# Attention outputs divided head by head, the first convolution tap on ScalarE, and four buffers for the backward states' loads

## The chip, the cores and the metric

The kernel runs on one core of a Trainium2 chip. The metric is the device time of one execution in microseconds, and of several executions the median. Everything is float32 in DRAM; matmul operands are split into a high and a low part (hi and lo), and three matmuls (hi hi, hi lo, lo hi) stand for one product of float32.

## The reference

One layer of a hybrid encoder block over 1024 tokens of width 1024. What matters here, cut down:

```
q, k, v, xBC, z, dt_raw, gates = split(h @ w_in)
# branch A, 16 heads of 64, 4 key heads
sc = einsum("bqgrd,bkgd->bgrqk", q, k) * scale
p = softmax(sc, axis=-1)
attn = einsum("bgrqk,bkgd->bqgrd", p, v)
# branch B
xBC = silu(depthwise_conv_centred(xBC, conv_w, conv_b))   # 5 taps, 3072 channels
ssd = ssd_mixer(...)                                       # chunked scan, forward and backward
merged = sigmoid(g_A) * (attn @ w_attn_out) + sigmoid(g_B) * (ssd @ w_ssd_out)
x = x + gate1 * (merged @ w_o)
...                                                        # then an MLP with squared relu
```

The softmax's division by the row sum is done on the output: the kernel forms exp(score - max) and its row sums, multiplies the unnormalised weights with v, and multiplies each output by the reciprocal of its row sum later.

## The kernel before, in words

The work runs through stages one after another, all in one program: modulation, the projections of q, k, v and z, then the three stages that the change touches, then the merge, w_o and the MLP. TensorE has most of the work. A scheduler puts the instructions of each engine in order when the program is built, from the order of the code and a timeline of its own; in attention and in the scan stage the order on TensorE alone is that of the code (manual_schedule), where weave mixes two streams by their costs. Each engine and each DMA queue works strictly in its order.

*Convolution stage (about 425 to 735 us).* 12 pairs of channel blocks of xBC, and one pair of gate blocks. A pair is one Strassen-Winograd step of the projection: its weights come in two loads, r0 (two buffers) and r1 (one buffer, so the next pair's load waits until the last reader of this one is through); GpSimd forms four sums of weight blocks (ws); each of seven operands is split into hi (ScalarE) and lo (VectorE for the plain blocks, GpSimd for the sums), both under the name wop, in four buffers; seven products of 12 matmuls follow (psc). VectorE and GpSimd add these into two rows pa and pb (both called pad, 1024 tokens and two zeros at either end). Then conv runs for pb and for pa: five taps. The first is L712 (pad times weight plus bias) and the other four are L715 (accumulator cacc plus shifted pad times weight), all five on VectorE; ScalarE applies SiLU in place, and a pair later TensorE turns the result to token order, eight transpositions that ScalarE copies out and stores to DRAM.

*Attention (about 735 to 1240 us).* 16 heads of 8 units of 128 queries. scores(u): four matmuls to pss, VectorE's negated row maximum (nm, L893), ScalarE's exponential (pf, L895) which also leaves the row sums in column u of zall. turn(u, hf): four transpositions (L906) to pst (two buffers), split into ph on ScalarE and pl on VectorE. values(b, hf), for blocks of four units: matmuls into pv (one buffer), whose two halves ScalarE (ax, L930) and VectorE (av) add up; av goes unnormalised to DRAM (av_d). Gate products (psg) are woven between. After the last unit, zall is turned at once, its reciprocals are formed, and stored to rz_d.

*Scan stage (from about 1240 us).* TensorE's order has the remaining gate products, the backward states of group 0 (bwd_stream: load xbb, two buffers, GpSimd's product xdb, one matmul, VectorE's update prevb, store pb), the scan of the chunks, and the product of attention's output with w_attn_out. load_a brings that output: for 16 tiles a load of av_d (araw, three buffers), two loads of rz_d that repeat a head's reciprocals over 64 partitions (rz, two buffers), VectorE's product, and the split into ah and al. All these loads stand in SP's one queue, which waits at an instruction whose buffer isn't free.

Of the kernel before, what the change touches and what calls it, by code (L numbers as in the profile page):

```python
# [18 lines left out]
P = 128  # L19
S = 1024  # L20
# [71 lines left out]
def block(ctx: ExitStack, tc: tile.TileContext, ia, out, upto=99, dbg=None):  # L92
# [611 lines left out]
    with tc.tile_pool(name="p2", bufs=1, reuse_waits="tile") as p2, \  # L704
# [4 lines left out]

        def conv(i, pad):  # L710
            acc = accs.pop() if accs else acc_tile()
            V.tensor_scalar(out=acc, in0=pad[:, 0:S], scalar1=cwT[:, i:i + 1], scalar2=vecT[:, CB0 + i:CB0 + i + 1],  # L712
                            op0=ALU.mult, op1=ALU.add)
            for k in range(1, 5):
                V.scalar_tensor_tensor(out=acc, in0=pad[:, k:k + S], scalar=cwT[:, 24 * k + i:24 * k + i + 1],  # L715
                                       in1=acc, op0=ALU.mult, op1=ALU.add)
            A.activation(acc, acc, AF.Silu)
# [130 lines left out]
    with tc.tile_pool(name="p3k", bufs=1, reuse_waits="tile") as p3k, \  # L848
# [11 lines left out]
        def attn_stream():  # L860
# [49 lines left out]
            pvs = {}  # L910

            def values(b, hf):

# [14 lines left out]
                if hf == 1:  # L928
                    ax = p3.tile([HD, 512], F32, name="ax", tag="ax", bufs=1)
                    A.copy(ax, pv[HD:])  # L930
                    av = p3.tile([HD, 512], F32, name="av", tag="av", bufs=2)
                    tt(V, av, ax, pv[:HD], ALU.add)
                    dma(av_d[h // 2][(h % 2) * HD:(h % 2 + 1) * HD, (b % 2) * 512:(b % 2 + 1) * 512], av)
                yield 0.92

            def all_values(b):
# [12 lines left out]
            for u in range(NU + 4):  # L949
                if u % NT == 4 and 1 < u // NT + 1 < NH:  # L950
                    load_head(u // NT + 1)
                if u + 2 < NU:
                    scores(u + 2)
                    yield 0.92
                for hf in range(2):
                    if u < NU:
                        turn(u, hf)
                        yield 0.44
                    if hf == 0:
                        c = next(pvq, None)  # L960
                        if c:
                            yield c
                if u % 4 == 3 and u < NU:
                    pvq = all_values(u // 4)
            ps = ps3.tile([P, 4, P], F32, name="pst", tag="pst", bufs=2)
            T.transpose(ps[:, 0], zall, ident)
            zt = p3.tile([P, P], F32, name="zt", tag="pf", bufs=2)
            V.reciprocal(zt, ps[:, 0])
            dma(rz_d.rearrange("h (a b) -> (h a) b", b=P), zt)

        with tc.manual_schedule(engines=M2):
            weave(tc, (attn_stream(), 128 * 2.72 + L0), (gates_stream(p3, ps3, 0, GATES_EARLY, 1, G), GATES_EARLY * 10.4), lead=LEAD2)
# [22 lines left out]
    with tc.tile_pool(name="p4", bufs=1, reuse_waits="tile") as p4, \  # L995
# [26 lines left out]
        def bwd_stream(g):  # L1022
            hs = slice(8 * g, 8 * g + 8)
            prev = None
            for c in range(7, 0, -1):
                xb = p4.tile([P, 640], F32, name="xbb", tag="xbb", bufs=2)
                dma(xb, xb_d[g][:, c])
                xt, bt = xb[:, 0:512].rearrange("p (h d) -> p h d", h=8), xb[:, 512:640]
                xd = p4.tile([P, 8, HD], F32, name="xdb", tag="xd", bufs=3)
# [113 lines left out]
        def load_a():  # L1143
            for half in range(2):
                ns = slice(half * 512, (half + 1) * 512)
                for k in range(KT):
                    raw = p4.tile([P, 512], F32, name="araw", tag="araw", bufs=3)
                    dma(raw, av_d[k][:, ns])
                    rz = p4.tile([P, 512], F32, name="rz", tag="rz", bufs=2)
                    for j in range(2):  # L1150
                        dma(rz[j * HD:(j + 1) * HD, :], rz_d[2 * k + j, ns].partition_broadcast(HD))
                    tt(V, raw, raw, rz, ALU.mult)
                    split(ahi[k][half], alo[k][half], raw)

        ghi, glo = act_tiles("g", KT)
# [552 lines left out]
```

## Time and profile before

| what | value |
|---|---|
| median of 3 runs | 2610.28 us (2604.86 to 2614.72) |
| the profiled execution | 2610.79 us, span 2608.8 us |
| mean granted TensorE clock | 0.975 |
| convolution, 456 to 717 us: TensorE, VectorE, GpSimd busy | 234.3, 219.2, 186.4 us |
| attention, 735 to 1240 us: TensorE, VectorE, ScalarE busy | 492.8, 335.8, 329.6 us |
| start of the scan, 1240 to 1330 us: TensorE busy, share of the DMA engines | 69.9 us, 0.82 |

PE is TensorE, DVE is VectorE, ACT is ScalarE, POOL is GpSimd; SPq and ACTq are the engines' DMA queues. A busy time says how long an engine had an instruction in hand, which for VectorE and GpSimd includes time in which the one holds the other up. A row of a group has line, engine, operation, out<-in by name, shapes and count, then busy time and the mean of one in nanoseconds, then idle time of that engine just before and what ended it. A row of the timeline has its start in us from the span's start, then its length. The chain of waits is followed back from the last instruction: each piece is what the next one waited for.

### The profile page before, as it was taken

The numbers are of one execution on the slowest core, as the hardware profiler recorded it, in microseconds if no ns is written. First come the engines' busy times: TensorE is split into PE (matmuls) and PEld (weight loads), VectorE is DVE, ScalarE is ACT, GpSimd is POOL, SyncE is SP. The second block draws the span as 40 slices with busy tenths as digits, with TensorE's granted clock in tenths as the row PEclk, the third lists the DMA queues.
The fourth block names the chain that finished last, engine by engine and source line by source line (L and its number), as shares of the span: only waits on it lengthen the run. The fifth ranks groups of instructions, "written<-read, shape, count | busy, mean of one in ns | idle before, by whom it ended". The sixth has DMA issues, their size and how long they took to land.

```text
span 2608.8 us, 32331 instructions
## 1 busy us (share of the span) xinstructions
PE 2435.3 (93%) x11340; PEld 1940.2 (74%) x11340; DVE 1844.4 (71%) x2200; ACT 1105.0 (42%) x1928; POOL 1016.0 (39%) x728
## 2 busy tenths in 40 slices
PE   5999999998989999999799999998989999899995
PEld 5998777776767777777567767776777888688884
DVE  5756347888856666666487787546569888768889
ACT  5455422333346666666233444343332222364441
POOL 2310117766710000000155666424018866633356
PEclk9999999999999999999899999999999999899998
DMA  7653741323441212111866675466315544754432
GB/s 258 184 157 124 253 152 61 89 85 93 145 140 45 77 45 79 47 52 29 239 216 196 194 223 169 125 221 207 133 49 178 189 144 144 265 179 149 142 93 97
DMA packets 286788, 369.69 MB, mean 142 GB/s; under 512 B 34201, under 2 KB 167041, under 8 KB 286625
## 3 DMA queue, kind: packets, MB, share of 16 engines
q1 hardware_dynamic: 215297, 292.62, 36.3%
q10 hardware_dynamic: 71328, 74.99, 8.7%
q8 instruction: 90, 1.47, 0.2%
q14 instruction: 73, 0.60, 0.1%
HBM read 251.33 MB, written 116.20 MB: 141 GB/s over the span
## 4 chain that ended last, share of the span: by engine, by line
PE 67%; DVE 11%; DMA 8%; issue 6%; POOL 5%; ACT 2%; SPq 1%; DVEq 0%; ACTq 0%; POOLq 0%
PE pst L906 5%; PE pp L1313 4%; PE pp L1315 4%; PE pp L1314 4%; PE psq L381 4%; PE psq L382 4%; PE psq L380 4%; PE psg L207 3%; PE psg L208 3%; PE psg L209 3%; PE p L1655 3%; PE p L1656 3%; PE p L1654 3%; PE pss L889 2%; PE pss L891 2%
## 5 line engine op out<-in xcount | busy, mean ns | idle before, releaser
L893 DVE TENSOR_REDUCE nm<-pss 128x1 f32<-128x1024 f32 x128 | 156.6, 1224 | 140.1 <-PE pss L891 139.6
L381 PE MATMUL psq<-twl,hh 128*128 128x400 f32 (+1 forms) x512 | 192.9, 378 | 5.9 <-DVE twl L155 4.1
L1655 PE MATMUL p<-o,o 128*128 128x512 f32 x448 | 179.8, 401 | 19.1 <-DVE o L155 19.1
L380 PE MATMUL psq<-twh,hh 128*128 128x400 f32 (+1 forms) x512 | 192.2, 381 | 3.7 <-ACT qkvr L513 1.2
L382 PE MATMUL psq<-twh,hl 128*128 128x400 f32 (+1 forms) x512 | 191.8, 377 | 0.0
L155 DVE TENSOR_TENSOR pl<-pst,ph 128x512 fp32r<-128x512 f32 x256 | 168.4, 684 | 27.5 <-ACT ph L169 27.5
L1654 PE MATMUL p<-o,o 128*128 128x512 f32 x448 | 177.3, 399 | 9.6 <-ACT o L169 7.7
L895 ACT ACTIVATE pf<-pss,nm 128x1024 f32<-128x1024 f32 x128 | 142.8, 1115 | 101.6 <-PE pst L906 98.0
L155 POOL TENSOR_TENSOR wlo<-wraw,whi 128x1024 fp32r<-128x1024 f32 x12 | 28.7, 2390 | 399.0 <-ACT whi L169 358.3
L1656 PE MATMUL p<-o,o 128*128 128x512 f32 x448 | 177.0, 397 | 0.0
L169 ACT CAST ph<-pst 128x512 fp32r<-128x512 f32 x256 | 146.3, 585 | 51.7 <-PE pst L906 37.5
L906 PEld LDWEIGHTS pst<-masks,pf 128*128 128x128 f32 x1024 | 118.8, 140 | 66.2 <-issue 28.8
L906 PE MATMUL pst<-masks,pf 128*128 128x128 f32 x1024 | 157.0, 276 | 9.7 <-DVE pl L155 9.6
L155 POOL TENSOR_TENSOR sl<-sl 128x512 f32<-128x512 f32 x64 | 95.0, 1492 | 175.5 <-DVE o L155 83.2
L715 DVE SCALAR_TENSOR_TENSOR cacc<-pad,cwT,cacc 128x1024 f32<-128x1024 f32 x96 | 149.7, 1570 | 0.4
L169 ACT CAST o<-ar 128x512 fp32r<-128x512 f32 x112 | 69.8, 623 | 175.8 <-PE p L1656 155.2
L155 DVE TENSOR_TENSOR o<-ar,o 128x512 fp32r<-128x512 f32 x112 | 107.2, 957 | 48.1 <-ACT o L169 48.1
L169 ACT CAST wop<-ws 128x512 fp32r<-128x512 f32 x116 | 70.6, 620 | 122.7 <-PE pp L1315 69.2
L1655 PEld LDWEIGHTS p<-o,o 128*128 128x128 f32 x448 | 86.5, 193 | 41.6 <-DVE o L155 23.7
L381 PEld LDWEIGHTS psq<-twl,hh 128*128 128x128 f32 x512 | 98.5, 192 | 17.9 <-DVE twl L155 5.2
L155 DVE TENSOR_TENSOR o<-sl,o 128x512 fp32r<-128x512 f32 x112 | 111.3, 994 | 0.1
L380 PEld LDWEIGHTS psq<-twh,hh 128*128 128x128 f32 x512 | 98.0, 192 | 16.0 <-ACT qkvr L513 1.7
(416 smaller groups left out, 7166.0 us busy)
## 6 DMA issues: line engine op xcount, KB each, us to landing
ar<-r SPq DMA_DIRECT2D x112, 256.0 KB
wada<-in_w_ada_dram SPq DMA_DIRECT2D x48, 512.0 KB
r<-in_w_mlp_dram SPq DMA_DIRECT2D x32, 512.0 KB
r<-as SPq DMA_DIRECT2D x64, 256.0 KB
sl<-in_w_mlp_dram SPq DMA_DIRECT2D x64, 256.0 KB
r<-in_w_in_dram SPq DMA_DIRECT2D x26, 512.0 KB
r<-ro ACTq DMA_DIRECT2D x48, 256.0 KB
xb<-cst ACTq DMA_DIRECT2D x20, 512.0 KB
```

The lines of the kernel that those rows point to most:

```text
L155: e.tensor_tensor(out=o, in0=a, in1=b, op=op)
L169: (e_hi or A.copy)(hi, src)
L380: T.matmul(o, hhi[k][half][:, sl], hi[:, k % 2, :n], start=k == 0, stop=False)
L381: T.matmul(o, hhi[k][half][:, sl], lo[:, k % 2, :n], start=False, stop=False)
L382: T.matmul(o, hlo[k][half][:, sl], hi[:, k % 2, :n], start=False, stop=k == KT - 1)
L715: V.scalar_tensor_tensor(out=acc, in0=pad[:, k:k + S], scalar=cwT[:, 24 * k + i:24 * k + i + 1], in1=acc, op0=ALU.mult, op1=ALU.add)
L893: V.tensor_reduce(out=nm, in_=ps, axis=AX.X, op=ALU.max, negate=True)
L895: A.activation(pfs[u], ps, AF.Exp, bias=nm, accum_out=zall[:, u:u + 1])
L906: T.transpose(pt[:, k], pf[:, (hf * 4 + k) * P:(hf * 4 + k + 1) * P], ident)
L1654: T.matmul(pss[t], a[:, 0, sl], b[:, 0], start=k == 0, stop=False)
L1655: T.matmul(pss[t], a[:, 0, sl], b[:, 1], start=False, stop=False)
L1656: T.matmul(pss[t], a[:, 1, sl], b[:, 0], start=False, stop=k == KR - 1)
```

## The change

Three parts. In the convolution the first tap goes from VectorE to ScalarE (Identity with scale and bias). In attention a head's reciprocals are formed as soon as its row sums stand: a reciprocal on VectorE over eight columns, a transposition of these to 8 x 128 on TensorE in a buffer of pst, a copy and a store on ScalarE's queue, one unit later a load over 64 partitions (rz, one buffer), and in the two units after that GpSimd multiplies the two halves of the head's output, which are then stored. load_a loads finished values and only splits them; the transposition of zall at the end goes. The backward states' load xbb gets four buffers instead of two.

```
-            V.tensor_scalar(out=acc, in0=pad[:, 0:S], scalar1=cwT[:, i:i + 1], scalar2=vecT[:, CB0 + i:CB0 + i + 1],
-                            op0=ALU.mult, op1=ALU.add)
+            A.activation(acc, pad[:, 0:S], AF.Identity, scale=cwT[:, i:i + 1], bias=vecT[:, CB0 + i:CB0 + i + 1])
...
+            def sums(h):
+                zi = p3.tile([P, NT], F32, name="zi", tag="zi", bufs=1)
+                V.reciprocal(zi, zall[:, NT * h:NT * h + NT])
+                pz = ps3.tile([P, 4, P], F32, name="pst", tag="pst", bufs=2)
+                T.transpose(pz[0:NT, 0], zi, ident)
+                zr = p3.tile([NT, P], F32, name="zr", tag="zr", bufs=1)
+                A.copy(zr, pz[0:NT, 0])
+                adma(rz_d[h].rearrange("(t p) -> t p", p=P), zr)
+            def sums_back(h):
+                rzs[h] = p3.tile([HD, S], F32, name="rz", tag="rz", bufs=1)
+                dma(rzs[h], rz_d[h].partition_broadcast(HD))
+            def divide(b):
+                h, av, hs = b // 2, avs.pop(b), slice((b % 2) * 512, (b % 2 + 1) * 512)
+                tt(G, av, av, rzs[h][:, hs], ALU.mult)
+                dma(av_d[h // 2][(h % 2) * HD:(h % 2 + 1) * HD, hs], av)
...
-                    dma(av_d[h // 2][(h % 2) * HD:(h % 2 + 1) * HD, (b % 2) * 512:(b % 2 + 1) * 512], av)
+                    avs[b] = av
...
+                h = u // NT - 1
+                if h >= 0:
+                    if u % NT == 0:
+                        sums(h)
+                    elif u % NT == 1:
+                        sums_back(h)
+                    elif u % NT in (2, 3):
+                        divide(2 * h + u % NT - 2)
...
-            ps = ps3.tile([P, 4, P], F32, name="pst", tag="pst", bufs=2)
-            T.transpose(ps[:, 0], zall, ident)
-            zt = p3.tile([P, P], F32, name="zt", tag="pf", bufs=2)
-            V.reciprocal(zt, ps[:, 0])
-            dma(rz_d.rearrange("h (a b) -> (h a) b", b=P), zt)
...
-                xb = p4.tile([P, 640], F32, name="xbb", tag="xbb", bufs=2)
+                xb = p4.tile([P, 640], F32, name="xbb", tag="xbb", bufs=4)
...
-                    rz = p4.tile([P, 512], F32, name="rz", tag="rz", bufs=2)
-                    for j in range(2):
-                        dma(rz[j * HD:(j + 1) * HD, :], rz_d[2 * k + j, ns].partition_broadcast(HD))
-                    tt(V, raw, raw, rz, ALU.mult)
```

The scheduler moves more than the lines that changed. VectorE in one round of the convolution, before, from the split of the next pair's second block to the split of its last (wop from r1): cacc_4406 belongs to pb (pad_4257), cacc_4430 to pa (pad_4254).

```order
L155 TENSOR_TENSOR wop_4465<-r1_4368,wop_4465 128x512
L712 TENSOR_SCALAR cacc_4406<-pad_4257,cwT_311,vecT_312 128x1024
L715 SCALAR_TENSOR_TENSOR cacc_4406<-pad_4257,cwT_311,cacc_4406 128x1024
L155 TENSOR_TENSOR pad_4254<-pad_4254,psc_4416 128x512
L715 SCALAR_TENSOR_TENSOR cacc_4406<-pad_4257,cwT_311,cacc_4406 128x1024
L712 TENSOR_SCALAR cacc_4430<-pad_4254,cwT_311,vecT_312 128x1024
L715 SCALAR_TENSOR_TENSOR cacc_4406<-pad_4257,cwT_311,cacc_4406 128x1024
L715 SCALAR_TENSOR_TENSOR cacc_4430<-pad_4254,cwT_311,cacc_4430 128x1024
L155 TENSOR_TENSOR wop_4532<-r1_4368,wop_4532 128x512
```

The same stretch now (a pair later; cacc_4589 belongs to pb, cacc_4613 to pa):

```order
L155 TENSOR_TENSOR wop_4648<-r1_4551,wop_4648 128x512
L155 TENSOR_TENSOR pad_4437<-pad_4437,psc_4599 128x512
L714 SCALAR_TENSOR_TENSOR cacc_4589<-pad_4440,cwT_311,cacc_4589 128x1024 x2
L714 SCALAR_TENSOR_TENSOR cacc_4613<-pad_4437,cwT_311,cacc_4613 128x1024
L714 SCALAR_TENSOR_TENSOR cacc_4589<-pad_4440,cwT_311,cacc_4589 128x1024
L155 TENSOR_TENSOR wop_4715<-r1_4551,wop_4715 128x512
```

The add of the last product to pa has moved ahead of all taps, and four taps instead of five and two first taps stand between it and the split. GpSimd in the same round, before: wop_4371 and wop_4413 are the lo parts of the pair's last two sums, ws_4443 is the next pair's first sum, which waits for the load of r1.

```order
L155 TENSOR_TENSOR wop_4371<-ws_4260,wop_4371 128x512
L775 MEMSET pad_4437 128x2
L776 MEMSET pad_4437 128x2
L155 TENSOR_TENSOR ws_4443<-r0_4366,r1_4368 128x512
L155 TENSOR_TENSOR wop_4413<-ws_4404,wop_4413 128x512
L155 TENSOR_TENSOR ws_4463<-ws_4443,r0_4366 128x512
```

And now:

```order
L155 TENSOR_TENSOR wop_4371<-ws_4260,wop_4371 128x512
L155 TENSOR_TENSOR wop_4413<-ws_4404,wop_4413 128x512
L155 TENSOR_TENSOR ws_4443<-r0_4366,r1_4368 128x512
L774 MEMSET pad_4437 128x2
L775 MEMSET pad_4437 128x2
L155 TENSOR_TENSOR ws_4463<-ws_4443,r0_4366 128x512
```

The lo part wop_4413 has moved from behind the sum that waits for r1 to ahead of it. ScalarE in attention, at the first unit of the second head, before (pst are turned blocks, pf exponentials):

```order
L169 CAST ph_6659<-pst_6661 128x4x128
L895 ACTIVATE pf_6657,zall_6042<-pss_6650,nm_6655 128x1024
L169 CAST ph_6659<-pst_6707 128x4x128
L169 CAST ph_6686<-pst_6688 128x4x128
L895 ACTIVATE pf_6702,zall_6042<-pss_6695,nm_6700 128x1024
```

And now, with the transposed reciprocals in pst_6707:

```order
L169 CAST ph_6669<-pst_6671 128x4x128
L894 ACTIVATE pf_6667,zall_6042<-pss_6660,nm_6665 128x1024
L918 COPY zr_6709<-pst_6707 8x128
L919 DMA rz_93<-zr_6709 8x128
L169 CAST ph_6669<-pst_6724 128x4x128
L169 CAST ph_6696<-pst_6698 128x4x128
L894 ACTIVATE pf_6719,zall_6042<-pss_6712,nm_6717 128x1024
```

The copy and the DMA issue stand behind the exponential and ahead of the two splits of turned blocks.

More of the change, by code (lines that the diff above doesn't have):

```diff
@@ L908, in turn @@
                 split(phs[b, hf][:, :, js], pls[b, hf][:, :, js], pt)
-            pvs = {}
+            pvs, rzs, avs = {}, {}, {}
+            def sums(h):
[13 more added lines that the diff above has]
+                dma(av_d[h // 2][(h % 2) * HD:(h % 2 + 1) * HD, hs], av)
             def values(b, hf):
```

## Prediction

> **What bounds the kernel now.** I read the busy shares first, then the chain that ended last.
>
> ```profile
> PE 2435.3 (93%) x11340; PEld 1940.2 (74%) x11340; DVE 1844.4 (71%) x2200; ACT 1105.0 (42%) x1928; POOL 1016.0 (39%) x728
> PE 67%; DVE 11%; DMA 8%; issue 6%; POOL 5%; ACT 2%; SPq 1%; DVEq 0%; ACTq 0%; POOLq 0%
> ```
>
> TensorE is busy for 93% of the span, yet only 67% of the chain is its own. So there are stretches that something else ends, and only there can this change gain. The busy times by stretch show which of its stages those are: the convolution (456 to 717 us), attention (735 to 1240) and the start of the scan (1240 to 1330).
>
> ```profile
> core 0: us, PE busy (x) PEld busy (x) DVE busy (x) ACT busy (x) POOL busy (x), PEclk, DMA share, GB/s
> 456.00:717.00 261.00, 234.30 (x1054) 188.34 (x1053) 219.16 (x188) 95.23 (x159) 186.36 (x153) 0.97 0.35 103
> 735.00:1240.00 505.00, 492.82 (x2595) 377.38 (x2594) 335.84 (x415) 329.62 (x578) 29.09 (x19) 1.00 0.20 59
> 1240.00:1330.00 90.00, 69.89 (x254) 48.31 (x252) 52.39 (x75) 24.07 (x43) 20.50 (x17) 0.89 0.82 243
> 1330.00:1690.00 360.00, 353.04 (x1694) 265.00 (x1695) 263.13 (x321) 143.40 (x293) 217.17 (x160) 1.00 0.61 185
> ```
>
> The convolution leaves TensorE 26.7 us idle, attention 12.2, the start of the scan 20.1. The waits of TensorE in the convolution, then one round of the chain there:
>
> ```profile
> PE psc L770 <- DVE wop L155: 20.3, 10, 2.3
> PE psc L770 <- POOL wop L155: 6.4, 6, 2.4
> ```
>
> ```profile
> 547.20 0.61 DVE wop L155
> ...
> 547.86 1.40 DMA r<-in_w_in_dram
> ...
> 551.75 1.98 POOL ws L155
> 553.73 1.70 POOL wop L155
> ...
> 560.71 1.06 POOL pad L155
> ...
> 561.79 1.57 DVE cacc L712
> ...
> 565.51 0.67 DVE pad L155
> ...
> 567.83 1.71 DVE cacc L712
> ...
> 571.92 0.61 DVE wop L155
> ```
>
> Read it as a ring. VectorE splits the last block of a pair (wop, ending at 547.81); only then is the single buffer r1 free and loaded; GpSimd can form the sums at 551.75 (3.94 us later); it ends the first pad at 561.77 (10.02); VectorE goes through two L712, five of the other operations and the next wop, ending at 572.53 (10.76). One round is 24.7 us, and in each TensorE waits about 2 us for that wop.
>
> **The convolution.** The change takes L712 out of the third leg. These rows give the prices: first two single taps, then groups of the stage.
>
> ```profile
> 538.67 2.19 DVE L715 SCALAR_TENSOR_TENSOR cacc<-pad,cwT,cacc 128x1024 f32<-128x1024 f32 x1
> 549.52 1.27 DVE L715 SCALAR_TENSOR_TENSOR cacc<-pad,cwT,cacc 128x1024 f32<-128x1024 f32 x1
> ```
>
> ```profile
> L155 POOL TENSOR_TENSOR wop<-ws,wop 128x512 fp32r<-128x512 f32 x44 | 87.9, 2017 | 0.0
> L155 POOL TENSOR_TENSOR pad<-pad,p 128x512 f32<-128x512 f32 x22 | 23.5, 1091 | 0.0
> L717 ACT ACTIVATE cacc<-cacc 128x1024 f32<-128x1024 f32 x21 | 22.3, 1061 | 128.6 <-DVE cacc L715 128.6
> ```
>
> A tap takes 1.27 us while GpSimd idles and 2.19 beside its work; a GpSimd operation of one shape takes 1.09 or 2.02. The two engines hold each other up, so what leaves VectorE's queue isn't simply saved. New round, leg by leg. Load: 3.94 unchanged. GpSimd: 10.02, less the wop of 1.70, which the new order puts ahead of the load's wait; but VectorE's add to the second pad now stands ahead of the first tap, so the second pad (1.09) and that add (0.67) come in: 10.08. ScalarE's tap has no row; its nearest is the SiLU over the same shape, 1.06 us, and it runs beside these 1.76 us, since it needs the first pad only. VectorE: four L715 and the wop (0.61), between 4 x 1.27 and 4 x 2.19, so 5.7 to 9.4; GpSimd now has four wop in a row there, so I take three taps at 2.19 and one at 1.27: 8.45. The round is 22.5 us (19.7 to 23.4).
>
> The second bound is TensorE: its 234.3 us over 10.6 rounds are 22.2 a round. So the gain a round is at most 2.5 us, at least 1.3, and I take 2.2. Of 12 pairs, the first and last lie outside the ring: 10 x 2.2 = 22 us gained. If the ring stays (below) it is 0; if all idle time and the lost clock (3% of 261 us) go, about 34.
>
> The tap's wait for the pad is new on ScalarE. Behind it stand the cast for the next product, the second tap and the copy of c1. ScalarE is busy for 95 of 261 us, and TensorE has a product of 12 matmuls in hand by then, so I cost that wait at nothing; were the cover gone, each round would give back up to the 1.06 us.
>
> The Trainium skill (SBUF — State Buffer, Who interferes with whom) says that VectorE with two SBUF inputs, or in a two-port mode as a scalar operation can be, and GpSimd hold one port pair in turn, for a whole instruction, and that ScalarE has ports of its own. By that rule eight taps, three wop and ten GpSimd operations lie end to end: about 22.9 us a round, an estimate with the alone prices above; the gain would be 18 us instead of 22.
>
> **Attention.** Per head the change adds a reciprocal, a small TensorE transposition, a copy and a DMA issue on ScalarE, a load on SP's queue, and two products on GpSimd.
>
> ```profile
> PE pst L906 <- DVE pl L155: 9.6, 17, 1.6
> L906 PE MATMUL pst<-masks,pf 128*128 128x128 f32 x980 | 150.2, 276 | 6.0 <-DVE pl L155 5.8
> L895 ACT ACTIVATE pf<-pss,nm 128x1024 f32<-128x1024 f32 x122 | 136.1, 1115 | 94.6 <-PE pst L906 93.2 <-DVE pl L155 0.9
> L895 ACT ACTIVATION_READ_ACCUMULATOR pf<-pss,nm 128x1 f32 x122 | 23.4, 192 | 0.0
> L930 ACT COPY ax<-pv 64x512 f32<-64x512 f32 x30 | 17.5, 583 | 12.3 <-PE pv L925 12.0
> 981.80 0.36 ACTq L856 DMA_DIRECT2D gt<-ost  x1
> ```
>
> TensorE is full here, so everything on it counts. A transposition of one block is 0.28 us at most, 16 of them 0 to 4.4 us; I take 2. It also takes one of two pst buffers, free again only after ScalarE's copy (0.19 to 0.58 us), which stands behind an exponential (1.12). The next turn needs that buffer after four score matmuls, about 0.9 us. So the wait lies between nothing and 1.12 + 0.58 + 0.36 - 0.9 = 1.2 us a head, 0 to 19 us. The exponential's scores were issued a whole unit earlier, so most of its time is past: I take 0.25 us a head, 4 us. The reciprocal stands ahead of two splits in VectorE's order, four units after its data; I cost it and the GpSimd products (32 x 1.09 us at most, in 505 us with 29 busy) at nothing. The loads move 16 x 256 KB into a stage whose DMA share is 0.20; SP holds q1 loads and stores behind each, needed units later. Sum: 6 us lost (2 to 23).
>
> **The start of the scan.** TensorE's waits there, what the DMAs moved, and the queue:
>
> ```profile
> PE psg L207 <- ACT ah L169: 8.4, 3, 4.3
> PE pst L1032 <- POOL xdb L155: 5.5, 1, 5.5
> PE psd L1082 <- ACT e L1085: 3.9, 1, 3.9
> PE psg L208 <- DVE al L155: 2.6, 2, 2.1
> ...
> ```
>
> ```profile
> DMA packets 16355, 22.38 MB, mean 231 GB/s; under 512 B 1814, under 2 KB 7390, under 8 KB 16350
> ...
> rz<-rz SPq DMA_DIRECT2D x32, 128.0 KB
> ...
> 1248.33 0.45 SPq L933 DMA_DIRECT2D av<-av  x1
> 1248.87 1.03 SPq L1027 DMA_DIRECT2D xbb<-xb  x2
> ...
> ```
>
> The 32 broadcast loads are 4.2 of 22.4 MB, 18 us at 231 GB/s, and 32 of the queue's issues; they leave, as do 16 VectorE products. The waits for ah and al (11.0 us) are waits for them, and the 5.5 us for xdb are a load of xbb that stood behind rz loads in SP's queue; with four buffers the first four are issued together. That is 16.5 us. The 3.9 us for e I leave. The clock is 0.89 over 90 us, about 10 us lost to half rate after these stalls; I take 4 back. Against it, SP now waits for the last head's division before the first xbb: transposition, store, load and product in a row, 2.5 us. Sum: 18 us gained; 6 if only waits for al and half of those for ah go, 28 if stalls and clock go whole.
>
> The later xbb loads of the backward states meet a stage in which TensorE is busy 353 of 360 us: nothing.
>
> **Sum.** 22 - 6 + 18 = 34 us gained. The profiled execution took 2610.8 us (span 2608.8), the median of before is 2610.3, so the forecast needs no shift: 2577 us.
>
> **Rivals.** *The ring stays.* GpSimd's fourth wop and the taps block each other for what was freed, and the convolution gives 0: 2610.8 + 6 - 18 = 2599. For it: the 2.02 against 1.09 us; against: the leg loses two operations of 1.6 us outright. 0.10.
>
> *The start stays DMA-bound.* The loads left are 18 MB, and states wait on each other through DRAM; only 3 us come back there: 2592. 0.08.
>
> *Slower.* The new slot wait in attention. If the copy stands behind its exponential and a reduction each time and the splits behind it come late as well, TensorE loses 3.5 us a head, 56 in all, against 40 gained: 2627. It decides from 2.5 us a head. Against it: TensorE's longest wait on pst is 1.6 us now, and 9.6 us over the whole stage. 0.07.
>
> *Everything clears.* Convolution 30, start 29 with its whole clock, attention 2 lost: 2554. 0.10. Whether the clock follows is open, as a gap of one round of the convolution shows:
>
> ```profile
> 547.85 0.50 PE L770 MATMUL psc<-u4h,wop 128*128 128x512 f32 x1 [2.26 <-DVE wop L155]
> ...
> 549.07 0.63 PE L768 MATMUL psc<-u4h,wop 128*128 128x512 f32 x1
> 549.50 0.63 PE L769 MATMUL psc<-u4l,wop 128*128 128x512 f32 x1
> ```
>
> After a gap of 2.26 us the matmuls start 0.43 us apart; the stage's mean is 234.3 / 1054 = 0.22 us. The Trainium skill (TensorE: Matmul & The Clock Gate, What's actually happening) halves the clock after an idle window of about 3.4 us. By that rule gaps of 2 us would cost no clock; the trace has half rate after one, so the measurement decides.
>
> That the change doesn't do what it says is no case: each moved instruction stands in the order.
>
> **Numbers.** The forecast has 0.65. Its own range: at best all three sums at their good ends, 25 + 28 - 2, gives 2560; their bad ends together would be 38 us worse, and I let one of them, or a bit under half of each, come true: 2594. Before's fastest run lies 5 us below its median, so 3 us more go below. With the two milder rivals (2592, 2599) the range 2557 to 2600 holds 0.83; left out are 2554 and 2627. A measurement of this kernel can tell about 0.5% (13 us) from no change: 2597 to 2623 is "same". Faster: forecast, start, clearing, less tails, 0.81; same 0.13 (the ring and tails); slower 0.06.
>
> **What would show it.** Right: TensorE's wait for wop in the convolution falls from 20 us to under 8 and the taps' rounds come every 22 to 23 us; waits on ah and al vanish; attention gets 2 to 10 us longer. Wrong: the round stays at 24, or pst waits pass 40 us in attention.

## The result, and the profile after

The changed kernel takes 2582.4 us (median of 4 runs, 2578.2 to 2585.6) where the kernel before took 2609.1 beside it. The ratio is 0.9895, with an interval of 0.9869 to 0.9922. Its profiled execution has a span of 2583.3 us, before 2608.8: 25.5 us less. The forecast was 34 us less, 2577, and a range of 2557 to 2600.

To see where the 25.5 us come from, I take five marks from TensorE's timeline, the same instructions in each kernel: the first psc matmul (convolution), the first pss (attention), the last pv (end of attention), the first psy (scan under way), the first psr (merge). The stretches between the marks, in us:

| stretch | before | after | difference | forecast |
|---|---|---|---|---|
| up to the first psc | 413.9 | 415.6 | +1.7 | 0 |
| convolution, first psc to first pss | 327.4 | 308.4 | -19.0 | -22 |
| attention, first pss to last pv | 504.0 | 509.2 | +5.2 | +6 |
| start of the scan, last pv to first psy | 75.9 | 65.8 | -10.1 | -18 |
| scan, first psy to first psr | 400.8 | 399.4 | -1.4 | 0 |
| the rest | 886.8 | 884.9 | -1.9 | 0 |

The first and the last row run over the same work in every kernel of this study. They came out between 411.0 and 416.0 us and between 882.6 and 889.9 us in them, so these two rows tell nothing. The page of the changed kernel:

```profile
PE 2435.1 (94%) x11355; PEld 1942.7 (75%) x11355; DVE 1835.2 (71%) x2175; ACT 1135.0 (44%) x1968; POOL 1047.2 (41%) x760
PE 69%; DVE 11%; DMA 8%; issue 5%; POOL 3%; ACT 3%; SPq 1%; ACTq 0%; DVEq 0%; POOLq 0%
```

Over the whole execution TensorE is as busy as before (2435 us); its idle time has become less. The busy times of the stretches between the marks, of before and then of the changed kernel (stretch, its length, then busy time and count for TensorE, its weight loads, VectorE, ScalarE and GpSimd, the granted clock, the DMA engines' share and GB/s):

```profile
413.90:741.30 327.40, 292.63 (x1284) 233.84 (x1283) 269.67 (x234) 114.97 (x188) 223.39 (x180) 0.96 0.36 110
741.30:1245.30 504.00, 492.24 (x2597) 376.55 (x2596) 337.95 (x417) 329.86 (x579) 28.59 (x18) 1.00 0.19 54
1245.30:1321.20 75.90, 57.49 (x198) 39.78 (x197) 43.32 (x64) 19.52 (x34) 15.52 (x14) 0.87 0.89 263
```

```profile
415.60:724.00 308.40, 285.19 (x1284) 231.29 (x1283) 260.58 (x210) 141.52 (x212) 214.14 (x180) 0.97 0.37 114
724.00:1233.20 509.20, 495.52 (x2612) 377.15 (x2611) 340.04 (x433) 332.24 (x595) 62.27 (x40) 1.00 0.21 63
1233.20:1299.00 65.80, 56.25 (x198) 39.12 (x197) 40.12 (x51) 19.84 (x35) 26.54 (x24) 0.90 0.81 262
```

Read the third line of each: the start of the scan moves data at 263 GB/s before and at 262 after. And read the first: 1284 matmuls, the same ones, keep TensorE busy for 292.6 us before and 285.2 after. So of the 19.0 us of the convolution 7.4 are busy time, and 11.6 are idle time (34.8 before, 23.2 after). Both will matter.

**The ring of the convolution.** One of its rounds in the changed kernel, from the chain that ended last:

```profile
543.58 0.61 DVE wop L155
...
544.24 3.72 DMA r<-in_w_in_dram
...
548.03 1.47 POOL ws L155
...
549.59 4.15 POOL ws L155 x3
...
554.77 2.49 POOL pad L155 x2
...
557.28 0.69 DVE pad L155
557.97 1.62 DVE cacc L714
...
559.62 2.27 DVE cacc L714 x2
...
563.98 2.31 DVE cacc L714
566.29 0.61 DVE wop L155
```

The legs are the forecast ones, in their new order: load 544.19 to 548.03 (3.84 us; forecast 3.94), GpSimd with VectorE's add 548.03 to 557.97 (9.94; 10.08), four taps and the split 557.97 to 566.90 (8.93; 8.45). The round is 22.7 us; 22.5 was forecast. ScalarE's first taps (1.25 us each, beside the second pad and the add) are not in the chain. But not every round is like that: from one matmul after this wait to the same one ten rounds later it is 708.26 - 474.89 us, 23.3 a round. The first nine take 23.0 on the mean (from 474.89 to 682.25 us) and the last 26.0. TensorE still waits for that split in nearly each:

```profile
PE psc L769 <- DVE wop L155: 16.9, 10, 2.6
PE psc L767 <- ACT hh L169: 2.9, 1, 2.9
PE psc L769 <- POOL wop L155: 1.6, 1, 1.6
```

**Attention.** The wait for the pst buffer that holds the turned reciprocals is there and small:

```profile
PE pst L905 <- DVE pl L155: 9.6, 17, 1.6
PE pst L905 <- ACT zr L918: 1.8, 4, 0.4
```

```profile
L916 PE MATMUL pst<-masks,zi x16: 272/273/276, 761.4 to 1229.5; 128*8 128x128 f32 x16
```

1.8 us in four waits for zr (forecast 4 us), and 3.3 us more of TensorE's busy time for the sixteen transpositions (forecast 2), together the 5.2 us.

**The start of the scan.** The wait for xdb (5.5 us) is gone, those for ah and al are not:

```profile
PE psg L207 <- ACT ah L169: 4.6, 3, 2.2
PE psd L1104 <- ACT e L1107: 3.2, 1, 3.2
PE psg L208 <- DVE al L155: 1.6, 3, 1.2
```

SP's queue shows why (start, length, then the instruction):

```profile
1236.29 1.90 SPq L929 DMA_DIRECT2D av<-av  x2
1238.28 1.98 SPq L1049 DMA_DIRECT2D xbb<-xb  x4
...
1251.31 1.33 SPq L1170 DMA_DIRECT2D araw<-av  x3
```

The first load of attention's output (araw) goes out 18.1 us after the last pv matmul (1233.2). The queue first waits for the last head's division, then come the four xbb loads and the loads of the scan. TensorE waits for ah because of araw now, where before it waited because of rz.

### The profile page after: what moved, and what is told of

Same layout as the page of the kernel before. It is cut to its first block, busy times and chain, and to the rows that moved or that the text cites. A ratio compares the mean times of both kernels' runs of the same rounds, so it can differ in the third digit from the quotient of the medians.

```text
span 2583.3 us, 32423 instructions
## 1 busy us (share of the span) xinstructions
PE 2435.1 (94%) x11355; PEld 1942.7 (75%) x11355; DVE 1835.2 (71%) x2175; ACT 1135.0 (44%) x1968; POOL 1047.2 (41%) x760
## 4 chain that ended last, share of the span: by engine, by line
PE 69%; DVE 11%; DMA 8%; issue 5%; POOL 3%; ACT 3%; SPq 1%; ACTq 0%; DVEq 0%; POOLq 0%
PE pst L905 5%; PE pp L1331 4%; PE pp L1333 4%; PE pp L1332 4%; PE psg L207 4%; PE psg L208 4%; PE psg L209 3%; PE psq L381 3%; PE psq L382 3%; PE psq L380 3%; PE p L1673 3%; PE p L1674 3%; PE p L1672 3%; DVE cacc L714 3%; PE pss L888 2%
## 5 line engine op out<-in xcount | busy, mean ns | idle before, releaser
L155 POOL TENSOR_TENSOR av<-av,rz 64x512 f32<-64x512 f32 x32 | 41.2, 1288 | 326.7 <-DMA rz<-rz 167.6
L714 DVE SCALAR_TENSOR_TENSOR cacc<-pad,cwT,cacc 128x1024 f32<-128x1024 f32 x96 | 162.9, 1727 | 0.4
L1673 PEld LDWEIGHTS p<-o,o 128*128 128x128 f32 x448 | 86.4, 193 | 42.0 <-DVE o L155 24.5
```

The source lines that it names most:

```text
L155: e.tensor_tensor(out=o, in0=a, in1=b, op=op)
L1673: T.matmul(pss[t], a[:, 0, sl], b[:, 1], start=False, stop=False)
```

## The experiments

The changed kernel and each experiment had the kernel before timed beside them; ratios are to that. Stretches are those of the table above, each from one profiled execution.

**The three parts one by one.** The first tap alone, in the kernel before:

```
-            V.tensor_scalar(out=acc, in0=pad[:, 0:S], scalar1=cwT[:, i:i + 1], ...)
+            A.activation(acc, pad[:, 0:S], AF.Identity, scale=cwT[:, i:i + 1], bias=...)
```

> The kernel before with only the first tap on ScalarE. My theory: the convolution's gain is this edit's alone, and nothing else in the program moves. From the first psc matmul to the first pss matmul the changed kernel needed 308.4 us where before needed 327.4; this kernel should need 307 to 311, and its time should be 15 to 21 us under before (ratio 0.992 to 0.994). Rival: part of those 19 us comes from the other edits, through the weights and gates loaded around the hand-over to attention; then this stretch is 312 us or more and the gain under 12 us.

The convolution's stretch is 308.1 us, as in the changed kernel: its gain is this edit's alone. The ratio is 0.9953 (0.9935 to 0.9971), 12 us, and not the 15 to 21 expected; in the profiled execution the scan was 5.5 us longer than before. Its trace has 2.6 us of new waiting for ah and 2.7 us more of TensorE's busy time there. Nothing in this edit explains either, and the cause stays open.

The division alone (the changed kernel with the tap on VectorE and two buffers for xbb):

```
-            A.activation(acc, pad[:, 0:S], AF.Identity, ...)
+            V.tensor_scalar(out=acc, in0=pad[:, 0:S], ...)
...
-                xb = p4.tile([P, 640], F32, name="xbb", tag="xbb", bufs=4)
+                xb = p4.tile([P, 640], F32, name="xbb", tag="xbb", bufs=2)
```

> The kernel before with only the division head by head (first tap on VectorE, two buffers for xbb). My theory: the 5.5 us stall on xdb came from rz loads that stood ahead of xbb loads in SP's queue, so it goes with the rz loads even with two buffers: attention 5 us longer as in the changed kernel, the stretch from the last pv matmul to the first psm matmul 8 to 11 us shorter than the 59.1 us before (it was 49.7 in the changed kernel), and the whole 3 to 6 us faster. Rival: the buffers were needed as well: the stretch is 54 us or more, and the whole is within 1 us of before or slower.

Ratio 0.9959 (0.9941 to 0.9976), 11 us faster: more than I expected. Attention takes 509.7 us, the stretch to the first psm matmul 50.9 (expected 48 to 51), and from there to the first psy it is 11.4 instead of 16.8. The stall on xdb hasn't gone, though, and there my theory fell: it is 10.3 us in this kernel, and those on ah are gone instead.

```profile
PE pst L1055 <- POOL xdb L155: 10.3, 3, 7.8
```

The four buffers alone:

```
-                xb = p4.tile([P, 640], F32, name="xbb", tag="xbb", bufs=2)
+                xb = p4.tile([P, 640], F32, name="xbb", tag="xbb", bufs=4)
```

> The kernel before with only four buffers for xbb. My theory: with the rz loads still in SP's queue the early xbb loads are issued together, so the 5.5 us stall on xdb goes, but the same bytes then delay the first ah: the stretch from the last pv matmul to the first psm matmul stays within 3 us of 59.1 and the whole within 4 us of before. Rival: the stall was the buffers' own and nothing takes its place: the stretch is 53 to 55 us and the whole 4 to 6 us faster.

Ratio 1.0016 (1.0004 to 1.0027): 4 us slower. The wait for xdb is gone, and those for ah and al have grown from 8.9 to 13.2 us. So the stall moves from one operand to the other, and the start of the scan doesn't get shorter: 76.8 us, before 75.9. That is under 1 of the 4 us. The rest lies in other stretches, and no run shows why.

The same from the other side, the changed kernel with two buffers:

```
-                xb = p4.tile([P, 640], F32, name="xbb", tag="xbb", bufs=4)
+                xb = p4.tile([P, 640], F32, name="xbb", tag="xbb", bufs=2)
```

> The changed kernel with two buffers for xbb again. My theory: the buffers bring nothing (alone they made the kernel before 4 us slower), so this one is within 4 us of the changed kernel's 2582, and a wait on xdb of 5 to 10 us stands where the changed kernel waits on ah. Rival: once the rz loads are gone the buffers are what removes the wait on xdb, and without them this kernel is 5 to 10 us slower than the changed one, 2587 to 2592.

2581.1 us, ratio 0.9875 (0.9856 to 0.9895): the same time as the changed kernel within the intervals. The start of the scan is 61.0 us instead of 65.8, though TensorE waits 8.6 us for xdb. So the third part of the change brought nothing, with or without the other two. By their ratios the three parts alone come to 12 + 11 - 4 = 19 us, and together to 27; the intervals are wide enough for that difference.

What the stretch moved stands in the DMA view of it (last pv to first psy), here of the changed kernel and of the one with two buffers:

```profile
DMA packets 12899, 17.24 MB, mean 262 GB/s; under 512 B 1208, under 2 KB 6338, under 8 KB 12894
```

```profile
DMA packets 12498, 16.38 MB, mean 269 GB/s; under 512 B 1163, under 2 KB 6288, under 8 KB 12493
```

| kernel | rz loads, xbb loads in the stretch | MB | GB/s | us |
|---|---|---|---|---|
| before | 31, 10 | 19.96 | 263 | 75.9 |
| four buffers alone | 31, 12 | 20.59 | 268 | 76.8 |
| changed kernel | 0, 12 | 17.24 | 262 | 65.8 |
| division alone | 0, 10 | 16.42 | 264 | 62.3 |
| changed, two buffers | 0, 10 | 16.38 | 269 | 61.0 |

The mean rate is 262 to 269 GB/s in all five, so bytes and time go together here. That alone doesn't say that the bytes set the time. The 31 rz loads were 4.06 MB, 15.4 us at 263 GB/s, and the change brought 10.1, since 1.34 MB of other transfers moved in. The four buffers put two more loads of 0.33 MB into the stretch, loads that otherwise go later. And the rate isn't one rate. These are the two parts of the stretch, up to the first psm matmul and from there to the first psy, of before and then of the changed kernel:

```profile
1245.30:1304.40 59.10, 44.74 (x154) 31.08 (x153) 29.18 (x44) 11.50 (x18) 11.46 (x10) 0.86 0.90 261
1304.40:1321.20 16.80, 12.74 (x45) 8.70 (x44) 14.14 (x21) 8.03 (x16) 4.06 (x4) 0.90 0.85 269
```

```profile
1233.20:1282.90 49.70, 43.40 (x153) 30.37 (x152) 29.12 (x35) 12.35 (x21) 24.21 (x22) 0.90 0.89 287
1282.90:1299.00 16.10, 12.85 (x46) 8.75 (x45) 11.00 (x16) 7.49 (x15) 2.33 (x2) 0.89 0.56 184
```

In the changed kernel the first part moves 287 GB/s and the second 184, with the DMA engines busy for 0.56 of it. So bytes may bound the first part, but hardly the second.

**Another queue for the loads.** If bytes decided, order wouldn't:

```
-                    dma(raw, av_d[k][:, ns])
+                    adma(raw, av_d[k][:, ns])
```

> The changed kernel with the loads of attention's output for w_attn_out (araw) issued on ScalarE's queue instead of SP's. My theory: the start of the scan is ended by the order in SP's one queue. There the first araw load stands behind the last head's stores and 20 loads of the scan and is issued 18 us after the last pv matmul; on another queue it goes at once, TensorE's waits for ah and al (6.2 us) go, and the stretch from the last pv to the first psm matmul falls from 49.7 to between 42 and 46 us. Rival, the bytes: the DMA engines are busy for 0.89 of that stretch, so the same bytes take the same time in whatever order; it stays within 2 us of 49.7, and waits for xdb or e take the place of those for ah. Third: ScalarE waits for buffers of araw ahead of its casts, and the stretch gets longer.

2584.2 us, ratio 0.9893 (0.9873 to 0.9913), no different from the changed kernel. The first araw load goes out 0.1 us after the last pv matmul, and the first part of the stretch, up to the first psm matmul, falls to 44.2 us, as the queue theory had it, with a wait for xdb in it now. But the part behind it grows from 16.1 to 19.3 us, with a wait for pbl:

```profile
PE pso L1122 <- DMA pbl<-pb: 3.6, 1, 3.6
PE pst L1054 <- POOL xdb L155: 3.0, 1, 3.0
```

The whole stretch is 63.5 us for 17.3 MB (272 GB/s), 297 GB/s in its first part and 216 in its second. The queue's order sets which operand is late, and the other order brought 2 us over the whole stretch, of the 4 to 8 expected up to the first psm matmul. What sets the rest is not shown: bytes in the first part, or the order in which states and operands wait on each other through DRAM.

**What holds the convolution's ring.** First whether the taps are held up by GpSimd. The low parts of the four sums become plain casts on ScalarE:

```
-                A.copy(t, product(w1_op(sm1, e_lo=G), H12))
+                A.copy(t, product(w1_op(sm1, e_lo=A), H12))
...
+        if e_lo is A:
+            A.copy(lo, src)
+            return
```

> The changed kernel, with the low parts of the four sums of a pair of the convolution taken from GpSimd: ScalarE writes them as a plain cast of the sum, so the subtraction of the high part is left out. My theory: the taps take 2.1 to 2.3 us instead of 1.27 because GpSimd's four splits run beside them. Without these, four taps fall from 8.4 to 5.1 us a round, TensorE's waits for wop fall from 17.8 us in all to under 5, and the stretch from the first psc to the first pss matmul falls from 308 to 293 to 298 us. Rival: the ring is held by the load of r1 and the chain of sums behind it, and the taps fit into slack: the stretch stays at 303 us or more though the taps get shorter. Third: the taps stay above 2 us, and then it isn't GpSimd's splits that hold them up.

The time of one run is 2545.3 us, the convolution's stretch 273.5: 35 us under the changed kernel, where I expected 10 to 15.

```profile
413.70:687.20 273.50, 272.82 (x1284) 227.10 (x1283) 216.69 (x209) 170.99 (x264) 121.19 (x128) 1.00 0.42 128
```

TensorE has no wait for wop left, and the clock is whole. The same 1284 matmuls are now 272.8 us of busy time. So the prediction's second bound, 22.2 us a round from TensorE's busy time, was no bound: a part of that busy time was matmuls at half rate behind the stalls. The taps' mean fell from 1.73 to 1.36 us. This run takes work from GpSimd and the hold from VectorE at once, so it doesn't yet tell the two apart.

Then whether the load of r1 is the leg to take out. A second buffer:

```
-                t = p2_tile("r1", [P, HK, 2, P], 1) if h and p else ...
+                t = p2_tile("r1", [P, HK, 2, P], 2) if h and p else ...
...
```

> The changed kernel with two buffers for r1 in the convolution. My theory, the ring: a round is load 3.9, GpSimd 9.2 and VectorE 9.6 us, one after the other because the load of r1 waits for VectorE's last split. With a second buffer the load leaves the ring; what is left is 18.8 us, less than TensorE needs (265.9 us for 13 pairs in the run without the low parts, 20.5 a pair), so the stretch from the first psc to the first pss matmul falls from 308 to between 275 and 285 us and the time to 2550 to 2562. Rival, the shared hold: VectorE and GpSimd hold each other up, and their work laid end to end at the prices of an undisturbed operation is 22.9 us a round whatever the order; then a round can't go under 22.9 from 23.4, and the stretch stays at 300 us or more.

It got slower: 2601.3 us, ratio 0.9956 (0.9941 to 0.9972), and the stretch 324.7 us instead of 308.4. My ring theory fell here, and the rival stood. The groups of the stage show how:

```profile
L714 DVE SCALAR_TENSOR_TENSOR cacc<-pad,cwT,cacc 128x1024 f32<-128x1024 f32 x96 | 180.7, 1912 | 0.4
```

```profile
L155 POOL TENSOR_TENSOR wop<-ws,wop 128x512 fp32r<-128x512 f32 x52 | 102.9, 1989 | 1.9 <-DVE cacc L714 1.5 <-ACT wop L169 0.4
```

And in the changed kernel:

```profile
L714 DVE SCALAR_TENSOR_TENSOR cacc<-pad,cwT,cacc 128x1024 f32<-128x1024 f32 x96 | 162.9, 1727 | 0.4
L155 POOL TENSOR_TENSOR wop<-ws,wop 128x512 fp32r<-128x512 f32 x52 | 92.1, 1783 | 18.2 <-ACT wop L169 18.0
```

The taps rose from 1.73 to 1.91 us, GpSimd's splits from 1.78 to 1.99. With the weights there early, GpSimd forms its sums while VectorE is at the taps: 67 of the 96 taps now lie beside GpSimd's work for over 80% of their length, in the changed kernel 37. The wait for the load had been useful: GpSimd stood still in it (5.5 us a round), and VectorE's taps of that time took 1.27 us. One thing isn't separated: the scheduler also gave GpSimd another order, sums and splits in turn, and rounds of 24.6 us are what both together made.

Next, less work for GpSimd, its two adds to the pads on VectorE:

```
-            tt(G, pb[:, H1], pb[:, H1], p5, ALU.add)
-            tt(G, pa[:, H1], pa[:, H1], p5, ALU.add)
+            tt(V, pb[:, H1], pb[:, H1], p5, ALU.add)
+            tt(V, pa[:, H1], pa[:, H1], p5, ALU.add)
```

> The changed kernel with GpSimd's two adds of the fifth product to the pads moved to VectorE. My theory, the ring: in each round of the convolution GpSimd's two adds (2.1 to 2.5 us) leave the leg between the sums and the taps and come back as two VectorE adds of 0.68 us, so a round gets 0.8 to 1.1 us shorter and the stretch from the first psc to the first pss matmul (308.3 us in the changed kernel) 9 to 13 us. Rival, VectorE is full: VectorE was busy for 260 of the 300 us of the convolution and the two adds push its splits back; the stretch stays within 4 us of 308 or gets longer.

2580.4 us, ratio 0.9878 (0.9861 to 0.9894); the stretch is 305.2 us, 3 less, as the rival had it. The adds aren't the 0.68 us that I took for them:

```profile
L155 DVE TENSOR_TENSOR pad<-pad,p 128x512 f32<-128x512 f32 x26 | 42.4, 1665 | 0.7 <-ACT p L808 0.6
```

They take 1.67 (the two that met no GpSimd work 0.69), while the adds with one input in PSUM (pad from psc) take 0.68 in the same stage. That gave the next theory, that only operations of VectorE with both inputs in SBUF are held up. The same adds, straight from PSUM:

```
-                t = p2_tile("p5", [P, 512], 1)
-                A.copy(t, product(w1_op(sm1, e_lo=G), H12))
-                return t
+                return product(w1_op(sm1, e_lo=G), H12)
...
```

> The changed kernel without ScalarE's copy of the fifth product; VectorE adds it to both pads straight from PSUM, and GpSimd's two adds go. My theory: VectorE and GpSimd hold each other up only where VectorE reads both inputs from SBUF. VectorE's adds with one input in PSUM took 0.68 us on the mean in every run so far, whatever GpSimd did, and its two adds from SBUF in the run with GpSimd's adds on VectorE took 1.67. So these two take 0.68 each, GpSimd has 2.2 us a pair less, and the stretch from the first psc to the first pss matmul falls from 308 to between 294 and 301 us; the time to 2568 to 2576. Rival: VectorE's queue as such is the limit, as the run with GpSimd's adds on VectorE suggests (305 us); then this one too stays at 303 us or more.

2564.6 us, ratio 0.9829 (0.9811 to 0.9847); the stretch is 286.6 us, 22 less than in the changed kernel and more than I expected. Against the run just above, where VectorE adds from SBUF, it is 18.6 less: the product read from PSUM and ScalarE's copy dropped. 65 adds from PSUM, the 26 new ones among them, take 0.68 us on the mean:

```profile
L155 DVE TENSOR_TENSOR pad<-pad,psc 128x512 f32<-128x512 f32 x65 | 43.0, 678 | 0.9 <-DVE pad L155 0.5
```

And the accumulator of the taps in PSUM:

```
-            acc = accs.pop() if accs else acc_tile()
+            acc = ps2.tile([P, S], F32, name="pacc", tag="pacc", bufs=1)
...
-            A.activation(acc, acc, AF.Silu)
+            y = acc_tile()
+            A.activation(y, acc, AF.Silu)
+            acc = y
...
-            ps = ps2.tile([P, 512], F32, name="psc", tag="psc", bufs=6)
+            ps = ps2.tile([P, 512], F32, name="psc", tag="psc", bufs=4)
```

> The changed kernel with the convolution's accumulator in PSUM: one buffer of two banks, for which the products keep four buffers instead of six; ScalarE's SiLU writes the result to SBUF. My theory: a tap that reads its accumulator from PSUM has one input in SBUF only and isn't held up by GpSimd, so the taps fall from 1.73 us on the mean to 1.3 to 1.5, GpSimd's splits from 1.78 towards 1.1, and the stretch from the first psc to the first pss matmul falls from 308 to between 285 and 300 us. Rival: any VectorE operation of that length is held up, wherever its inputs lie: the taps stay above 1.65 us and the stretch at 306 us or more. Third: the taps get shorter, but TensorE waits more than 15 us for buffers of PSUM (the four for products, the one for the accumulator), and the stretch stays above 300 us.

2553.3 us, ratio 0.9783 (0.9767 to 0.9800); the stretch is 280.7 us.

```profile
L714 DVE SCALAR_TENSOR_TENSOR pacc<-pad,cwT,pacc 128x1024 f32<-128x1024 f32 x96 | 123.4, 1285 | 5.2 <-ACT pacc L712 3.7
L155 DVE TENSOR_TENSOR wop<-r,wop 128x512 fp32r<-128x512 f32 x37 | 30.3, 818 | 2.5 <-ACT wop L169 1.8
```

```profile
PE psc L769 <- ACT hh L169: 4.0, 1, 4.0
PE psg L207 <- ACT ost L856: 0.7, 1, 0.7
```

The taps take 1.285 us, what an undisturbed tap takes, though GpSimd works beside them: the 53 taps that lie beside its work for over 80% of their length take 1.28 us. The 37 such taps of the changed kernel took 1.87. GpSimd's splits fall from 1.78 to 1.39 us, and the 37 of them beside which VectorE had no operation with two inputs in SBUF take 1.29. TensorE waits for no wop in the whole convolution, and for none of its PSUM buffers (psc, pst). So the theory stands for the taps and the adds: one input in PSUM frees them. That two inputs in SBUF are the only case of the hold it doesn't show. In the kernel before, the first tap (L712) has one input row, in SBUF, and took 0.80 us where no GpSimd work met it and 1.56 to 1.78 in 22 of its other 23 executions.

**Attention without the turn.** VectorE's reciprocals go to DRAM in turned order, with no transposition:

```
-                pz = ps3.tile([P, 4, P], F32, name="pst", tag="pst", bufs=2)
-                T.transpose(pz[0:NT, 0], zi, ident)
...
-                adma(rz_d[h].rearrange("(t p) -> t p", p=P), zr)
+                adma(rz_d[h].rearrange("(t p) -> p t", p=P), zi)
```

> The changed kernel without the small transposition and the copy in attention: the 128 x 8 reciprocals are stored straight from VectorE's tile, by a store that writes 1024 values of four bytes in the turned order. My theory: attention's 5.2 us are 16 transpositions (3.3 us more of TensorE's busy time) and 1.8 us of waits for zr, so attention falls from 509.3 to 503 to 505 us and the whole by 3 to 6 us against the changed kernel (2573 to 2581). Rival: the store of single values takes so long that the division of the last head comes later; then the stretch from the last pv to the first psm matmul grows from 49.7 by 3 us or more and nothing is gained.

Attention is 505.1 us, at the end of what was expected, so the price of the turn is 4.2 us. But the whole is 2582.8 us, ratio 0.9893 (0.9871 to 0.9915): no gain to be seen, in an interval of about 6 us to either side. The last head's store goes out at 1216.8 us, and the load of it, which waits for it to land, only at 1228.2:

```profile
L915 ACTq DMA_DIRECT2D rz<-zi x1: 377/377/377, 1216.8 to 1216.8; - x1
L920 SPq DMA_DIRECT2D rz<-rz x1: 463/463/463, 1228.2 to 1228.2; - x1
```

That is 11.4 us (9.1 to 12.0 over the 16 heads); in the changed kernel the store of turned rows goes out at 1230.1 and the load at 1231.4. So the last division is late, its store leaves SP's queue 7.6 us after the last pv matmul instead of 3.0, and the stretch from the last pv to the first psm matmul grows by 2.1 us. Up to the first psy matmul it is 65.8 us in both, so the trace doesn't show where the 4.2 us would have gone; in the profiled executions this kernel is 3.4 us shorter.

**Together.** Accumulator in PSUM, no turn, two buffers:

> The changed kernel with three edits together: the convolution's accumulator in PSUM, the reciprocals stored straight from VectorE's tile in place of the small transposition, and two buffers for xbb. My theory, that the three stages add up: 2553 us with the accumulator in PSUM alone, less 4.2 us in attention (505.1 us there in place of 509.3), less some 4 us at the start of the scan, where the stretch from the last pv to the first psy matmul was 61 to 62 us in both kernels with the division and two buffers and 64.5 to 66 in those with four: 2545 us, 2542 to 2549. Rival: what is saved ahead of the start of the scan is given back there, as in the run without the small transposition, whose attention was 4.2 us shorter and whose time was that of the changed kernel: then the time is 2550 to 2556, no better than with the accumulator alone.

2551.2 us, ratio 0.9770 (0.9750 to 0.9790): the rival's case, the same as with the accumulator alone within the intervals. Attention is 504.8 us, but the start of the scan is 65.0 instead of 61 to 62 (64.5 with the accumulator alone): the last head's store goes out 6.0 us after the last pv matmul, the stretch moves 256 GB/s, and one wait for xdb is 10.2 us.

```profile
PE pst L1052 <- POOL xdb L155: 12.8, 2, 10.2
```

The version to keep is the changed kernel with the accumulator in PSUM, 57 us under before.

## Why the prediction came out as it did

*The convolution* (forecast 22, measured 19). Right in the legs of the round: the gain is this edit's alone, and the tap on ScalarE stands in no link of the chain. The typical round was forecast at 22.5 us and is 22.7. The term is a little too big because the mean of ten rounds is 23.3. But the sign named for it didn't come: TensorE's wait for wop was to fall from 20 to under 8 us, and 16.9 are left. Of the 19.0 us gained 7.4 are busy time of the same matmuls, which the prediction took as fixed.

*TensorE as the second bound* (22.2 us a round). This step failed, without harm to the sum. The run with the low parts cast on ScalarE needs 20.5 us a pair (265.9 us from the first psc to the last, for 13 pairs). The prediction took busy time for work; some of it was half rate. The clock records show when: the half rate comes in pieces of 3.41 us. Laid on a grid of that length in the convolution of before and of the changed kernel, each piece at full rate in which TensorE was busy for 0.44 or less was followed by half rate (11), and none in which it was busy for 0.47 or more. A gap of 2 us can fill that much of one piece or fall across two, which is why some gaps were followed by half rate and others not.

*The hold between VectorE and GpSimd.* Taken from the trace as 1.27 against 2.19 us, it was priced about right (four taps and the split 8.93 against 8.45). The rule of one port pair in turn (the Trainium skill, SBUF — State Buffer, Who interferes with whom) gave 22.9 us a round as an estimate, and 18 us of gain. The convolution's 19.0 us lie nearest to that, but by luck. The estimate took 1.09 us for each of ten GpSimd operations; that is the price of its two adds, and its splits and sums take 1.29 where no two-input VectorE operation meets them. With that price for eight of the ten the estimate is 24.5 us a round, and the rounds measured are shorter (23.3). So the two engines' operations hold each other up, and yet don't lie end to end in full. The trace with a second buffer for r1 agrees in kind, since there an earlier load made more of both engines' work meet. The same section of the Trainium skill says that a VectorE instruction with at most one SBUF input, outside the two-port modes, doesn't take part. The adds from PSUM (0.68 us) and the taps on an accumulator in PSUM (1.285 us) agree.

*Attention* (forecast 6 lost, measured 5.2). Right in its total, with the parts the other way round: 3.3 us for the transpositions and 1.8 of waits, where 2 and 4 were forecast, so that the two errors cancel is luck. The rival of 3.5 us a head lost nothing like that: four waits of about 0.4 us each.

*The start of the scan* (forecast 18, measured 10.1). This term was mis-sized. The step "The waits for ah and al (11.0 us) are waits for them" failed. In the stretch from the last pv to the first psy those waits were 8.9 us before, and 6.2 are left without any rz load: 2.7 us came back, and the waits now end with loads of araw. The wait for xdb gave its 5.5 us as forecast, that for e 0.7, and TensorE's busy time 1.2 where 4 were taken for the clock; together 10.1. The reason given for xdb failed too: with the rz loads gone and two buffers it is 10.3 us. And "with four buffers the first four are issued together" is true but no gain: it only traded the wait for xdb against waits for ah and al. The rival that the start stays DMA-bound was right that most of the loads' waits stay; it was wrong in its price, 3 us, and in the part after the first psm matmul the DMA engines are busy for 0.56 of the time. What does set the length of this stretch stays open.

*The sum* (forecast 34, measured 25.5 by the spans, 27 by the medians) is short by the 8 us of the start and the 3 of the convolution; attention and the other stretches gave some 2 back. The stretches behind changed by less than 2 us, so nothing was given back there.

## What to carry to other kernels

Where VectorE and GpSimd share a stage, look first at which VectorE operations read both inputs from SBUF; keeping an accumulator in PSUM, or adding a product before it is copied out, which also took two adds from GpSimd, was worth more here (29 and 18 us, on top of the change) than moving a whole tap to another engine (12). Before taking a load out of a ring, ask which engine its wait keeps quiet. In a stretch that loads fill, don't add up the stalls: when one is taken away, another operand is the late one. And look at the GB/s of its parts before calling it bound by bytes.

## What the runs showed of the hardware

- TensorE's busy time for the same 1284 matmuls was 292.6, 285.2 and 272.8 us, at granted clocks of 0.96, 0.97 and 1.00: gaps of about 2 us in nearly every round cost more than their own length.
- A VectorE add of 128 x 512 took 1.67 us with both inputs in SBUF and 0.68 with one in PSUM, beside GpSimd work in the same stage.
- A tap of 128 x 1024 beside GpSimd work took 1.87 us with its accumulator in SBUF and 1.28 with it in PSUM; with no GpSimd work beside it, 1.27 and 1.29.
- A store of 1024 values of four bytes took 9 to 12 us until its load could start; the store of the same values as eight rows took 1.2 to 1.4 for 15 of the 16 heads.
- Four loads issued at once in place of two, with nothing else changed, took TensorE's wait for one operand and raised that for another from 8.9 to 13.2 us.
